# Down projection with stored activation sums: seven-product pairs at nine positions of each group instead of seven

## The chip, the cores and the metric

One Trainium2 chip, one of its cores. The metric is the device time of one execution in microseconds; lower is better. Engines: TensorE (PE, with its weight loads PEld), VectorE (DVE), ScalarE (ACT), GpSimd (POOL) and SyncE (SP); GpSimd and SyncE here mostly issue transfers.

## The reference

One layer (DEPTH 1) over 256 positions of width 2048, float32. A mixer comes first (its projection, gated chunks, neighbourhood attention, gates, output projection). Then a channel mixer, which is what the change touches, and a final norm:

```python
def conv_ffn(x, g_norm, w_up, conv_k, conv_b, w_down):      # D_FF = 5504, so 43 blocks of 128
    h = rms_norm(x, g_norm)
    up = h @ w_up                                            # 256 x 2048 by 2048 x 11008
    ...                                                      # centred depthwise convolution, width 3
    gate, val = jnp.split(up, 2, axis=-1)
    return x + (jax.nn.silu(gate) * val) @ w_down            # 256 x 5504 by 5504 x 2048
```

## The kernel before

**Products in two halves.** Every float32 operand is split into a high half (ScalarE copies it, rounding: `whi`, line 151) and a low half (VectorE subtracts the high half from the original: `wlo`, line 152). A product is a *triple* of matmuls (`triple`, lines 289 to 293): high by high, low by high, high by low.

**Order.** The schedule is written out by hand. All weights are a list of *pieces* that is worked from front to back. `begin(i)` opens piece `i`: it issues the load of the piece four further on (`load_to`, five `wraw` buffers, SyncE's queue, lines 126 and 132), splits the piece three further on (`split_to`, four `whi` and four `wlo` buffers), and runs the tasks registered for `i` with `at(i, f)`. Each engine works its instructions in the order in which they were issued this way, so a task that is put into a later piece stands behind that piece's splits. A tile that is allocated again under its name waits until its last reader is through.

**Up projection** (`g_up`, lines 199 to 221). 22 groups of eight pieces, weights stationary, two feature blocks (a *pair*, the last group one block) with gate and value in each. `ev_up` then brings the results out: banks to `ta` (lines 979 and 981), and as tasks convolution (987 to 994), SiLU and product (999 and 1000), and the split into the activation tile `a` (`split_plain`, 485 and 486). First block: one to three pieces after the group's end; second: three to five.

**Down projection** (`g_dn`, `wide`, `run_wide`). Two groups of 1024 output columns. A piece is one feature block (128 rows of `w_down`) by 1024 columns, two halves of 512; positions are two tiles of 128. A group has 43 pieces: 21 pairs of pieces at positions 0 to 20, and one left over. A *plain* pair takes 2 x 2 x 2 = 8 triples. At the positions in `DOWN_QUADS` the pair is done as a 2 x 2 block product with seven multiplications instead of eight (7 triples), by block sums of the activations and of the weights:

- `act_sums` (lines 295 to 304, five pieces ahead) adds the activation's halves back together and makes four block sums; `act_sums_split` (306 to 311, four ahead) splits them, into the tiles `h6` and `h7` of the pool `hT`.
- `weight_sums` (313 to 319, three ahead) makes four sums of the raw weight blocks, `weight_sums_split` (322 to 330, two ahead) splits them. Of the two pieces themselves, the first is then split only by half (`units`).
- The seven products go into the group's four banks and four banks of their own; `ev_sums` (899 to 922) adds the latter to the residual `x2` in two halves, `first_half` one piece and `second_half` two pieces after the last such pair.

The last four pieces of the second group are worked block by block (positions tile by column half, `tail` in `run_wide`), and `finish` ends each block: residual, squares, gain, and for each tile the norm and the output. `ev_down` ends the first group: residual, squares and gains of its columns, and `load_fin` (line 1272), which loads gains through GpSimd's queue into one of two buffers.

The same sums (`act_sums`, `weight_sums`, `post_sums`, `add_sums`) serve the four other places where seven products are used: the projection's `v` and values, the gates and the output projection.

Of the kernel before, what the change touches and what calls it, by code (L numbers as in the profile page):

```python
# [8 lines left out]
F32 = mybir.dt.float32  # L9
# [15 lines left out]
NF = DFF // 128  # L25
# [30 lines left out]
OUT_ORDER = (tuple(range(16)), (0, 1, 6, 7, 2, 3, 10, 11, 4, 5, 8, 9, 12, 13, 14, 15))  # L56
TURN_X2 = (13, 1)
Y_GAP = 224
DOWN_QUADS = ((4, 6, 9, 11, 14, 16, 18), (3, 5, 8, 10, 13, 15, 17))


@with_exitstack
def trunk_kernel(ctx, tc, x, norm_mix, w_in, ln_g, ln_b, w_s, b_s, rpb, w_branch, w_out,
# [200 lines left out]

    def wide(src, row0, order, c0, acts, quads, room, done, sums=None, odd=None):
        n0 = plan_wide(src, row0, order, c0)
        boxes = {}
        for n, q in enumerate(quads):  # L270
            i = n0 + 2 * q
            own = odd if odd and n % 2 else room
            whole[i] = whole[i + 1] = None
            units[i], units[i + 1] = 1, 2
            b = boxes[q] = {}
            if sums is None:
                b["acts"] = {}
                sum_acts_at(i - 5, i - 4, b["acts"], lambda k=order[2 * q]: ff["ap"][k // 2], room, "s")
            else:
                b["acts"] = sums[order[2 * q]]  # L280
            at(i - 3, lambda i=i, b=b: weight_sums(i, b, room))
            at(i - 2, lambda b=b, own=own: weight_sums_split(b, own))
        return ("wide", n0, order, acts, quads, boxes, done)
# [5 lines left out]
    def triple(p, x, h, l, st, sp):  # L289
# [2 lines left out]
        nc.tensor.matmul(p, xl, h, start=False, stop=False)  # L292
        nc.tensor.matmul(p, xh, l, start=False, stop=sp)  # L293

    def act_sums(a, box, room):
        w = room("f", F32)
        f = w[:, 0].rearrange("p (k t) -> p k t", k=2)
        nc.vector.tensor_add(f, a[:, :, 0, :].bitcast(F32), a[:, :, 1, :].bitcast(F32))
        s1, s2, s3, s4 = (w[:, 1, n * 128:(n + 1) * 128] for n in range(4))
        nc.vector.tensor_add(s1, f[:, 0, 128:], f[:, 1, 128:])  # L300
        nc.vector.tensor_sub(s3, f[:, 0, :128], f[:, 0, 128:])
        nc.vector.tensor_sub(s2, s1, f[:, 0, :128])
        nc.vector.tensor_sub(s4, f[:, 1, :128], s2)
        box["w"] = w

    def act_sums_split(box, room, name):
        w = box.pop("w")
        o = room(name, F32R)
        nc.scalar.activation(o[:, 0], w[:, 1], AF.Copy)
        nc.vector.tensor_sub(o[:, 1], w[:, 1], o[:, 0].bitcast(F32))  # L310
        box["s"] = [(o[:, 0, n * 128:(n + 1) * 128], o[:, 1, n * 128:(n + 1) * 128]) for n in range(4)]

    def weight_sums(i, box, room):
        r0, r1 = whole.pop(i), whole.pop(i + 1)
        t13, t24 = room("t13", F32), room("t24", F32)
        nc.vector.tensor_sub(t13[:, 0], r0[:, 1], r0[:, 0])
        nc.vector.tensor_sub(t24[:, 0], r1[:, 1], t13[:, 0])
        nc.vector.tensor_sub(t13[:, 1], r1[:, 1], r0[:, 1])
        nc.vector.tensor_sub(t24[:, 1], r1[:, 0], t24[:, 0])
        box["w"] = (t13, t24)  # L320

    def weight_sums_split(box, room):
        u = []
        for name, t in zip(("13", "24"), box.pop("w")):
            h, l = room("h" + name, F32R), room("l" + name, F32R)
            nc.scalar.activation(h, t, AF.Copy)
            nc.vector.tensor_sub(l, t, h.bitcast(F32))
            u.append((h, l))
        box["t"] = {1: [x[:, 0] for x in u[0]], 3: [x[:, 1] for x in u[0]],
                    2: [x[:, 0] for x in u[1]], 4: [x[:, 1] for x in u[1]]}  # L330

    def run_wide(g, tail=0):
        kind, n0, order, acts, quads, boxes, done = g
        n1 = n0 + len(order)
        P = C = None

        def x_of(k, t):
            a = acts(k)
            return a[:, 0, t * 128:(t + 1) * 128], a[:, 1, t * 128:(t + 1) * 128]

        def plain(i, t, c):
            h, l = split_t[i]
            triple(C[t][c], x_of(order[i - n0], t), h[:, c], l[:, c], i == n0, i == n1 - 1)

        for i in range(n0, n1 - tail):
            begin(i)
            q, r = divmod(i - n0, 2)
            if C is None:
                c = [bank() for _ in range(4)]
                C = [c[:2], c[2:]]  # L350
            if q not in quads:
                for t, c in ((0, 0), (0, 1), (1, 0), (1, 1)) if i > 1 else ((0, 0), (1, 0), (0, 1), (1, 1)):
                    plain(i, t, c)
                split_t.pop(i)
                continue
            st, sp = q == quads[0], q == quads[-1]
            k, k1 = order[2 * q:2 * q + 2]
            if r == 0:
                if st:
                    P = [bank() for _ in range(4)]  # L360
                (h0, l0), (h1, l1) = split_t[i], split_t[i + 1]
                triple(P[0], x_of(k, 0), h0[:, 0], l0[:, 0], st, sp)
                triple(C[0][0], x_of(k1, 0), h1[:, 0], l1[:, 0], False, False)
                triple(C[0][1], boxes[q]["acts"]["s"][3], h1[:, 1], l1[:, 1], False, False)
                split_t.pop(i)
                split_t.pop(i + 1)
                continue
            S, W = boxes[q]["acts"]["s"], boxes[q]["t"]
            triple(P[1], S[0], *W[1], st, sp)
            triple(P[3], S[2], *W[3], st, sp)  # L370
            triple(P[2], S[1], *W[2], st, sp)
            triple(C[1][0], x_of(k1, 1), *W[4], False, False)
            if sp:
                done[0](P, i)
        if not tail:
            done[1](C, n1)
            return
        for t in range(NT):
            for c in range(2):
                for i in range(n1 - tail, n1):  # L380
                    if t == 0 and c == 0:
                        begin(i)
                    plain(i, t, c)
                done[1](C, t, c)
# [140 lines left out]
    def post_sums(P, x, spare):  # L525
        p1, p5, p6, p7 = P
        (x11, x12), (x21, x22) = x
        nc.scalar.activation(x11, p1, AF.Copy)
        nc.vector.tensor_add(spare, p6, x11)
        nc.vector.tensor_add(x12, p5, spare)  # L530
        nc.vector.tensor_add(x21, p7, spare)
        nc.vector.tensor_add(x22, p5, x21)

    def add_sums(ps, x):
        for t in range(NT):
            for c in range(2):
                nc.vector.tensor_add(x[t][c], ps[t][c], x[t][c])

    def ev_v_sums(P, i):
        def go():  # L540
# [358 lines left out]
    def ev_sums(j, room):  # L899
        def done(P, i):  # L900
# [5 lines left out]
            def first_half():  # L906
                ab, cd = room("t13", F32), room("t24", F32)
                m["v"], m["u3"], m["w"] = cd[:, 0], cd[:, 1], ab[:, 0]
                nc.scalar.activation(ab[:, 0], p1, AF.Copy)
                nc.vector.tensor_add(x11, p1, x11)  # L910
                nc.vector.tensor_add(ab[:, 1], p6, ab[:, 0])
                nc.vector.tensor_add(m["v"], p5, ab[:, 1])
                nc.vector.tensor_add(m["u3"], p7, ab[:, 1])
                nc.vector.tensor_add(m["w"], p5, m["u3"])

            def second_half():
                nc.vector.tensor_add(x12, x12, m["v"])
                nc.vector.tensor_add(x21, x21, m["u3"])
                nc.vector.tensor_add(x22, x22, m["w"])

            at(i + 1, first_half)
            at(i + 2, second_half)
# [50 lines left out]
    def ev_up(f0, nb):  # L973
        def done(ps, i):
            n = nb
            a = []
            for p in ps:
                t = tmp.tile([128, T], F32, name="tb", bufs=3)
                nc.scalar.activation(t, p[:, T:], AF.Copy)  # L979
# [18 lines left out]
            def gate(b, g, v):  # L998
                nc.scalar.activation(g, g, AF.Silu)
                nc.vector.tensor_mul(g, g, v)  # L1000
                at(cur[0] + 1, lambda: split_plain(g, ff["a"][f0 + b]))

            at(i + 1, lambda: conv(0))
            if n > 1:
# [19 lines left out]
    def ev_down(ps, i):  # L1024
# [8 lines left out]
        def columns(j):  # L1033
            for t in range(NT):
                scale_columns(t, j)
            fin["load"]()

        for j in range(2):
            at(i + 2 + j, lambda j=j: squares(j))
# [93 lines left out]
    for f in range(0, NF, 2):  # L1133
        nb = min(2, NF - f)
        g_up.append(stationary(w_u, 0, KD, f * 128, nb * 128, 2, DFF, lambda k: rs["h", k], ev_up(f, nb)))
    h_room = {n: f"h{i}" for i, n in enumerate(("t13", "t24", "h13", "h24", "l13", "l24", "f", "s"))}

    def down_room(name, dt):
        return hpool.tile([128, 2, 512], dt, name=h_room[name])

    g_dn = [wide(w_d, 0, range(NF), g * 1024, lambda k: ff["a"][k], DOWN_QUADS[g], down_room,
                 (ev_sums(2 * g, down_room), ev_down if g == 0 else finish)) for g in range(2)]


    preload[0] = [lambda: load_x(0, 256)]
    for n, (c, _) in enumerate(X_TURN[1:]):
# [102 lines left out]
    ctx.push(fa_st)  # L1249
    ff["ap"] = [fa.tile([128, min(2, NF - k), 2, T], F32R, name=f"a{k // 2}") for k in range(0, NF, 2)]  # L1250
    ff["a"] = [ff["ap"][k // 2][:, k % 2] for k in range(NF)]
    fc = {}

    def open_conv():
# [54 lines left out]
```

## Time and profile before

| | |
|---|---|
| three runs, median | 1316.88 us (1316.34 to 1316.91) |
| profiled execution, span from first to last instruction | 1314.9 us; no other time of its own is given |
| mean granted TensorE clock | 0.998 |
| instructions | 19329 |
| weight transfers of the down projection, `in_w_down_dram` | 86 x 512 KB, median 4.6 us to landing |
| device memory read, written | 253.90 MB, 2.10 MB |

The span is about 2 us less than the runs' times. Rows of a profile table of windows give the stretch, its length, and then the busy time (and instructions) of PE, PEld, DVE, ACT and POOL, the granted clock, the transfer engines' share and GB/s. Rows of the timeline give start, duration, engine, line, operation, output<-inputs, shape, and in brackets the idle time before with what ended it. Rows of the waits give the waiting engine and line, what it waited for, and the time in all, the times and the longest. Durations of successive instructions on one engine overlap by about 0.1 us, so starts are the surer measure.

### The profile page before, as it was taken

What the parts mean: (1) busy time and instruction counts of PE and PEld (TensorE: products, weight loads), DVE (VectorE), ACT (ScalarE), POOL (GpSimd) and SP (SyncE); (2) the same over time, 40 slices, a digit from 0 to 9 for tenths busy, and PEclk for the clock granted to TensorE, in tenths of its full rate; (3) what the DMA queues carried; (4) which work ended last, traced back from release to release, by engine and by line L of the source; (5) the groups of instructions that cost most, each with busy time, mean ns of one, the idle gap of its engine ahead of it and who ended that gap; (6) DMA issues with size and microseconds to landing.
All of it is one profiled execution on the core that took longest, in us unless ns stands there. A gap on an engine that the chain in (4) does not pass through costs nothing.

```text
span 1314.9 us, 19329 instructions
## 1 busy us (share of the span) xinstructions
PE 1303.3 (99%) x6776; PEld 1112.0 (85%) x6776; DVE 1066.2 (81%) x1625; ACT 764.8 (58%) x1139; POOL 88.3 (7%) x176
## 2 busy tenths in 40 slices
PE   9999999999999999999999999999999999999997
PEld 7888888888888888888888888888888888888885
DVE  7996778667789966986777778787878789999997
ACT  5766476666645644556555555555656556555653
POOL 0004505323000000000000000000000000000000
PEclk9999999999999999999999999999999999999999
DMA  8768656556556657665565665656565656666663
GB/s 305 260 209 235 201 174 201 181 163 194 179 172 209 210 190 241 204 210 163 175 202 182 192 193 182 195 184 193 180 205 177 198 154 226 220 194 206 210 202 119
DMA packets 170577, 259.37 MB, mean 197 GB/s; under 512 B 12664, under 2 KB 124144, under 8 KB 170480
## 3 DMA queue, kind: packets, MB, share of 16 engines
q1 hardware_dynamic: 166448, 250.31, 59.4%
q0 software_dynamic: 3712, 7.30, 2.4%
q8 instruction: 53, 0.87, 0.3%
q10 hardware_dynamic: 320, 0.53, 0.1%
q14 instruction: 44, 0.36, 0.1%
HBM read 253.90 MB, written 2.10 MB: 195 GB/s over the span
## 4 chain that ended last, share of the span: by engine, by line
PE 97%; DVE 1%; ACT 0%; issue 0%; DMA 0%; ACTq 0%; DVEq 0%
PE bank L205 31%; PE bank L209 16%; PE bank L293 12%; PE bank L291 12%; PE bank L292 12%; PE bank L233 5%; PE bank L235 4%; PE bank L234 4%; PE bank L761 1%; DVE wlo L152 0%; PE bank L811 0%; PE bank L503 0%; PE bank L627 0%; PE bank L801 0%; PE bank L892 0%
## 5 line engine op out<-in xcount | busy, mean ns | idle before, releaser
L152 DVE TENSOR_TENSOR wlo<-wraw,whi 128x1024 fp32r<-128x1024 f32 (+1 forms) x472 | 550.3, 1178 | 188.7 <-ACT whi L151 92.0
L151 ACT ACTIVATE whi<-wraw 128x1024 fp32r<-128x1024 f32 (+1 forms) x472 | 472.0, 1015 | 204.7 <-PE bank L292 75.2
L205 PE MATMUL bank<-h,whi 128*128 128x512 f32 x1760 | 426.0, 392 | 0.0
L205 PEld LDWEIGHTS bank<-h,whi 128*128 128x128 f32 x1760 | 321.9, 188 | 62.0 <-DVE ya L631 0.3
L209 PEld LDWEIGHTS bank<-h,wlo 128*128 128x128 f32 x1760 | 225.9, 191 | 8.8
L209 PE MATMUL bank<-h,wlo 128*128 128x256 f32 x1760 | 228.6, 283 | 0.0
L989 ACT ACTIVATE tc<-ta,ck 128x256 f32<-128x256 f32 x86 | 47.1, 594 | 117.1 <-DVE ta L987 117.1
L293 PE MATMUL bank<-wlo,a 128*128 128x512 f32 x260 | 101.5, 390 | 0.2 <-DVE wlo L152 0.2
L292 PE MATMUL bank<-whi,a 128*128 128x512 f32 x260 | 101.2, 389 | 0.0
L291 PE MATMUL bank<-whi,a 128*128 128x512 f32 x260 | 101.2, 389 | 0.0
L291 PE MATMUL bank<-whi,h 128*128 128x512 f32 x204 | 80.3, 393 | 0.0
L292 PE MATMUL bank<-whi,h 128*128 128x512 f32 x204 | 79.5, 390 | 0.0
L293 PE MATMUL bank<-wlo,h 128*128 128x512 f32 x204 | 79.5, 390 | 0.0
L293 PEld LDWEIGHTS bank<-wlo,a 128*128 128x128 f32 x260 | 48.8, 188 | 11.2 <-DVE wlo L152 1.3
L292 PEld LDWEIGHTS bank<-whi,a 128*128 128x128 f32 x260 | 48.8, 188 | 10.3
L291 PEld LDWEIGHTS bank<-whi,a 128*128 128x128 f32 x260 | 48.8, 188 | 10.1
L992 DVE SCALAR_TENSOR_TENSOR tc<-ta,ck,tc 128x255 f32<-128x255 f32 x86 | 41.4, 481 | 14.5 <-ACT tc L989 14.5
L979 ACT ACTIVATE tb<-bank 128x256 f32<-128x256 f32 x86 | 28.3, 385 | 42.2 <-PE bank L205 42.2
L233 PE MATMUL bank<-whi,y 128*128 128x512 f32 x128 | 50.5, 394 | 0.0
L233 PE MATMUL bank<-whi,h 128*128 128x512 f32 x128 | 50.4, 394 | 0.0
L235 PE MATMUL bank<-wlo,h 128*128 128x512 f32 x128 | 49.9, 390 | 0.0
L235 PE MATMUL bank<-wlo,y 128*128 128x512 f32 x128 | 49.9, 390 | 0.0
(299 smaller groups left out, 1744.1 us busy)
## 6 DMA issues: line engine op xcount, KB each, us to landing
wraw<-in_w_up_dram SPq DMA_DIRECT2D x336, 256.0 KB, 3.2
wraw<-in_w_in_dram SPq DMA_DIRECT2D x111, 512.0 KB, 4.5
wraw<-in_w_down_dram SPq DMA_DIRECT2D x86, 512.0 KB, 4.6
wraw<-in_w_in_dram SPq DMA_DIRECT2D x66, 256.0 KB, 3.2
wraw<-in_w_branch_dram SPq DMA_DIRECT2D x32, 512.0 KB, 4.5
wraw<-in_w_out_dram SPq DMA_DIRECT2D x32, 512.0 KB, 3.6
xs<-in_x_dram SPq DMA_DIRECT2D x8, 256.0 KB, 7.6
vw<-y POOLq DMA_DIRECT2D x16, 128.0 KB, 6.9
```

Of the source, the lines that this page charges most:

```text
L151: nc.scalar.activation(h[:, k, :m], w[:, k, :m], AF.Copy)
L152: nc.vector.tensor_sub(l[:, k, :m], w[:, k, :m], h[:, k, :m].bitcast(F32))
L205: nc.tensor.matmul(p, h[:, k - k0, b * 128:(b + 1) * 128], acts(k), start=k == 0, stop=k == nk - 1)
L209: nc.tensor.matmul(p[:, :T], l[:, k - k0, b * 128:(b + 1) * 128], acts(k)[:, 0, :], start=False, stop=False)
L233: nc.tensor.matmul(p, xh, h[:, kk, :m], start=st, stop=False)
L234: nc.tensor.matmul(p, xl, h[:, kk, :m], start=False, stop=False)
L235: nc.tensor.matmul(p, xh, l[:, kk, :m], start=False, stop=sp)
L291: nc.tensor.matmul(p, xh, h, start=st, stop=False)
L292: nc.tensor.matmul(p, xl, h, start=False, stop=False)
L293: nc.tensor.matmul(p, xh, l, start=False, stop=sp)
L989: nc.scalar.activation(v, u, AF.Identity, scale=ck[:, 1, ch:ch + 1], bias=ck[:, 3, ch:ch + 1])
L992: nc.vector.scalar_tensor_tensor(v[:, 1:], u[:, :T - 1], ck[:, 0, ch:ch + 1], v[:, 1:], op0=OP.mult, op1=OP.add)
```

## The change

The block sums of the activations are no longer made in the down projection, once for each group. For nine pairs of feature blocks (3, 5, ... 19) they are made once, in the up projection: two pieces after the second block's gate VectorE makes the four sums from the unsplit product, one piece later they are split, and GpSimd's queue stores them in device memory (512 KB for each pair). The down projection loads them through the same queue, four pieces ahead of the pair, into `h6` and `h7` in turn. Both groups have nine seven-product pairs, at every second position; in the second group the blocks are put in another order, so that the stored pairs stand at its positions. The block sums are written with other signs (`act_blocks`, `weight_sums`), and the places that take them follow. The gain load after the first group is put three pieces later. GpSimd's descriptor space falls from its default to 4096 bytes a partition, and a pool `more` holds the sums on their way.

```diff
-DOWN_QUADS = ((4, 6, 9, 11, 14, 16, 18), (3, 5, 8, 10, 13, 15, 17))
+DOWN_PAIRS = (3, 5, 7, 9, 11, 13, 15, 17, 19)
+DOWN_QUADS = (DOWN_PAIRS, (2, 4, 6, 8, 10, 12, 14, 16, 18))
...
-            if sums is None:
+            if stored:
                 b["acts"] = {}
-                sum_acts_at(i - 5, i - 4, b["acts"], lambda k=order[2 * q]: ff["ap"][k // 2], room, "s")
+                at(i - 4, lambda b=b, k=order[2 * q]: stored(k // 2, b["acts"]))
...
+    def act_blocks(w, a11, a21, a12, a22):
+        s3, n1, p2, s4 = (w[:, n * 128:(n + 1) * 128] for n in range(4))
+        nc.vector.tensor_sub(s3, a11, a21)
+        nc.vector.tensor_sub(n1, a22, a21)
+        nc.vector.tensor_add(p2, n1, a11)
+        nc.vector.tensor_sub(s4, a12, p2)
...
-        nc.vector.tensor_sub(t13[:, 0], r0[:, 1], r0[:, 0])
-        nc.vector.tensor_sub(t24[:, 0], r1[:, 1], t13[:, 0])
-        nc.vector.tensor_sub(t13[:, 1], r1[:, 1], r0[:, 1])
-        nc.vector.tensor_sub(t24[:, 1], r1[:, 0], t24[:, 0])
+        nc.vector.tensor_add(t13[:, 0], r0[:, 0], r0[:, 1])
+        nc.vector.tensor_add(t24[:, 1], t13[:, 0], r1[:, 1])
+        nc.vector.tensor_add(t13[:, 1], r0[:, 1], r1[:, 1])
+        nc.vector.tensor_add(t24[:, 0], r1[:, 0], t24[:, 1])
...
-            triple(P[1], S[0], *W[1], st, sp)
-            triple(P[3], S[2], *W[3], st, sp)
-            triple(P[2], S[1], *W[2], st, sp)
+            triple(P[1], S[1], *W[1], st, sp)
+            triple(P[3], S[0], *W[3], st, sp)
+            triple(P[2], S[2], *W[2], st, sp)
...
                 at(cur[0] + 1, lambda: split_plain(g, ff["a"][f0 + b]))
+                own[b] = g
+                if b and f0 // 2 in ff["kept"]:
+                    at(cur[0] + 2, sums)
+                    at(cur[0] + 3, sums_split)
+
+            def sums():
+                own["w"] = ff["more"].tile([128, 512], F32, name="sw")
+                act_blocks(own["w"], *(own[k][:, t * 128:(t + 1) * 128] for k in range(2) for t in range(2)))
+
+            def sums_split():
+                o = ff["more"].tile([128, 2, 512], F32R, name="so")
+                split_plain(own["w"], o)
+                nc.gpsimd.dma_start(ff["kept"][f0 // 2], o.bitcast(F32))
...
-            fin["load"]()
+            at(cur[0] + 3, fin["load"])
...
-    h_room = {n: f"h{i}" for i, n in enumerate(("t13", "t24", "h13", "h24", "l13", "l24", "f", "s"))}
+    h_room = {n: f"h{i}" for i, n in enumerate(("t13", "t24", "h13", "h24", "l13", "l24", "s0", "s1"))}
...
-    g_dn = [wide(w_d, 0, range(NF), g * 1024, lambda k: ff["a"][k], DOWN_QUADS[g], down_room,
-                 (ev_sums(2 * g, down_room), ev_down if g == 0 else finish)) for g in range(2)]
+    def stored(pair, box):
+        n = ff["turn"] = ff.get("turn", -1) + 1
+        o = down_room(f"s{n % 2}", F32R)
+        nc.gpsimd.dma_start(o.bitcast(F32), ff["kept"][pair])
+        box["s"] = sums_of(o)
+
+    def down_order(g):
+        free = [p for p in range(NF // 2) if p not in DOWN_PAIRS]
+        kept = list(DOWN_PAIRS)
+        pairs = [(kept if q in DOWN_QUADS[g] else free).pop(0) for q in range(NF // 2)]
+        return tuple(2 * p + kk for p in pairs for kk in range(2)) + (NF - 1,)
+
+    g_dn = [wide(w_d, 0, down_order(g), g * 1024, lambda k: ff["a"][k], DOWN_QUADS[g], down_room,
+                 (ev_sums(2 * g, down_room), ev_down if g == 0 else finish), stored=stored) for g in range(2)]
+    dram = keep("dram", space=bass.MemoryType.DRAM)
+    ff["kept"] = {p: dram.tile([128, 2, 512], F32, name=f"sums{p}") for p in DOWN_PAIRS}
...
-    nc = _bacc.Bacc("TRN2", target_bir_lowering=False, num_devices=1)
+    nc = _bacc.Bacc("TRN2", target_bir_lowering=False, num_devices=1, dynamic_dma_scratch_size=4096)
```

The lines left out turn the signs where the sums are taken up (`post_sums`, `add_sums`, `ev_sums`: one subtraction for one addition), and divide `act_sums` into `act_blocks` and the rest.

More of the change, by code (lines that the diff above doesn't have):

```diff
@@ L262, in run_group, with wide @@
             done(ps, b)
-    def wide(src, row0, order, c0, acts, quads, room, done, sums=None, odd=None):
+    def wide(src, row0, order, c0, acts, quads, room, done, sums=None, odd=None, stored=None):
         n0 = plan_wide(src, row0, order, c0)
@@ L298, in act_sums @@
         nc.vector.tensor_add(f, a[:, :, 0, :].bitcast(F32), a[:, :, 1, :].bitcast(F32))
[L299 to L303, printed above, removed]
+        act_blocks(w[:, 1], *(f[:, k, t * 128:(t + 1) * 128] for k in range(2) for t in range(2)))
         box["w"] = w
@@ L310, in act_sums_split, with sums_of @@
         nc.vector.tensor_sub(o[:, 1], w[:, 1], o[:, 0].bitcast(F32))
-        box["s"] = [(o[:, 0, n * 128:(n + 1) * 128], o[:, 1, n * 128:(n + 1) * 128]) for n in range(4)]
+        box["s"] = sums_of(o)
+    def sums_of(o):
+        return [(o[:, 0, n * 128:(n + 1) * 128], o[:, 1, n * 128:(n + 1) * 128]) for n in range(4)]
     def weight_sums(i, box, room):
@@ L329, in weight_sums_split @@
         box["t"] = {1: [x[:, 0] for x in u[0]], 3: [x[:, 1] for x in u[0]],
-                    2: [x[:, 0] for x in u[1]], 4: [x[:, 1] for x in u[1]]}
+                    2: [x[:, 1] for x in u[1]], 4: [x[:, 0] for x in u[1]]}
     def run_wide(g, tail=0):
@@ L528, in post_sums @@
         nc.scalar.activation(x11, p1, AF.Copy)
-        nc.vector.tensor_add(spare, p6, x11)
+        nc.vector.tensor_sub(spare, x11, p6)
         nc.vector.tensor_add(x12, p5, spare)
@@ L536, in add_sums @@
             for c in range(2):
-                nc.vector.tensor_add(x[t][c], ps[t][c], x[t][c])
+                (nc.vector.tensor_sub if c else nc.vector.tensor_add)(x[t][c], ps[t][c], x[t][c])
     def ev_v_sums(P, i):
@@ L910, in first_half @@
                 nc.vector.tensor_add(x11, p1, x11)
-                nc.vector.tensor_add(ab[:, 1], p6, ab[:, 0])
+                nc.vector.tensor_sub(ab[:, 1], ab[:, 0], p6)
                 nc.vector.tensor_add(m["v"], p5, ab[:, 1])
@@ L916, in second_half @@
             def second_half():
-                nc.vector.tensor_add(x12, x12, m["v"])
+                nc.vector.tensor_sub(x12, x12, m["v"])
                 nc.vector.tensor_add(x21, x21, m["u3"])
-                nc.vector.tensor_add(x22, x22, m["w"])
+                nc.vector.tensor_sub(x22, x22, m["w"])
             at(i + 1, first_half)
@@ L976, in done @@
             a = []
+            own = {}
             for p in ps:
@@ L1135, in trunk_kernel @@
         g_up.append(stationary(w_u, 0, KD, f * 128, nb * 128, 2, DFF, lambda k: rs["h", k], ev_up(f, nb)))
-    h_room = {n: f"h{i}" for i, n in enumerate(("t13", "t24", "h13", "h24", "l13", "l24", "f", "s"))}
+    h_room = {n: f"h{i}" for i, n in enumerate(("t13", "t24", "h13", "h24", "l13", "l24", "s0", "s1"))}
     def down_room(name, dt):
         return hpool.tile([128, 2, 512], dt, name=h_room[name])
-    g_dn = [wide(w_d, 0, range(NF), g * 1024, lambda k: ff["a"][k], DOWN_QUADS[g], down_room,
-                 (ev_sums(2 * g, down_room), ev_down if g == 0 else finish)) for g in range(2)]
+    def stored(pair, box):
+        n = ff["turn"] = ff.get("turn", -1) + 1
+        o = down_room(f"s{n % 2}", F32R)
+        nc.gpsimd.dma_start(o.bitcast(F32), ff["kept"][pair])
+        box["s"] = sums_of(o)
+    def down_order(g):
[7 more added lines that the diff above has]
+    ff["kept"] = {p: dram.tile([128, 2, 512], F32, name=f"sums{p}") for p in DOWN_PAIRS}
     preload[0] = [lambda: load_x(0, 256)]
@@ L1251, in trunk_kernel @@
     ff["a"] = [ff["ap"][k // 2][:, k % 2] for k in range(NF)]
+    ff["more"], more_st = pool("more")
+    ctx.push(more_st)
     fc = {}
```

## The prediction
> **What bounds the kernel now.** I read the page's busy times and chain first, then a table of two windows (up projection, down projection), then what the matmul and weight-load queues wait for in each.
>
> ```profile
> PE 1303.3 (99%) x6776; PEld 1112.0 (85%) x6776; DVE 1066.2 (81%) x1625; ACT 764.8 (58%) x1139; POOL 88.3 (7%) x176
> PE 97%; DVE 1%; ACT 0%; issue 0%; DMA 0%; ACTq 0%; DVEq 0%
> ...
> 606.00:1080.00 474.00, 474.00 (x2730) 419.02 (x2729) 364.78 (x602) 271.76 (x436) 0.00 (x0) 1.00 0.59 185
> 1080.00:1315.00 235.00, 225.58 (x992) 185.61 (x991) 218.87 (x323) 128.59 (x162) 2.21 (x4) 0.99 0.60 198
> ...
> PEld bank L293 <- DVE wlo L152: 1.3, 3, 0.6
> PE bank L293 <- DVE wlo L152: 0.2, 1, 0.2
> ```
>
> TensorE is 97% of the chain. The last two rows are all it waits for from 1080 us on, and between 606 and 1080 it waits for nothing. The window rows give the room beside it: VectorE has 109 us left of 474 in the up projection (77% busy), but is 93% busy in the down projection. So matmuls taken out of the down projection count in full, as long as VectorE's low halves still arrive ahead of them. A busy matmul row overlaps the next one, so I take the pace from starts instead: these rows are the first matmul of the pair at position 4 and of the pair at position 6, the first two seven-product pairs, with one plain pair between.
>
> ```profile
> 1103.63 0.39 PE L291 MATMUL bank<-whi,h 128*128 128x512 f32 x1
> 1113.83 0.39 PE L291 MATMUL bank<-whi,h 128*128 128x512 f32 x1
> ```
>
> A seven-product pair has 7 triples, a plain pair 8: 21 + 24 = 45 matmuls in 10.20 us, 0.2267 us each.
>
> **Term 1, the matmuls.** Seven-product pairs go from 7 + 7 to 9 + 9. Four more pairs, one triple less each: 12 x 0.2267 = 2.72 us off TensorE. The other groups keep their matmuls; only signs change there, at one instruction for one (the block sums in `act_blocks` have one more back-to-back dependence, 0.1 us each time on VectorE, hidden).
>
> **Term 2, VectorE and ScalarE in the down projection.** Starts in order, from 1093.67 us:
>
> ```profile
> 1093.67 0.68 DVE L298 TENSOR_TENSOR h<-a 128x512 f32<-128x512 f32 x1
> 1094.39 0.29 DVE L300 TENSOR_TENSOR h<-h 128x128 f32<-128x128 f32 x1
> ...
> 1095.33 0.42 DVE L486 TENSOR_TENSOR a<-tc,a 128x256 fp32r<-128x256 f32 x1
> 1096.80 0.69 DVE L310 TENSOR_TENSOR h<-h,h 128x512 fp32r<-128x512 f32 x1
> 1097.40 0.69 DVE L152 TENSOR_TENSOR wlo<-wraw,whi 128x512 fp32r<-128x512 f32 x1
> 1098.00 0.69 DVE L316 TENSOR_TENSOR h<-wraw 128x512 f32<-128x512 f32 x1
> ...
> 1100.54 1.22 DVE L152 TENSOR_TENSOR wlo<-wraw,whi 128x1024 fp32r<-128x1024 f32 x1
> 1101.68 2.35 DVE L327 TENSOR_TENSOR h<-h,h 128x1024 fp32r<-128x1024 f32 x2
> 1103.95 1.22 DVE L152 TENSOR_TENSOR wlo<-wraw,whi 128x1024 fp32r<-128x1024 f32 x1
> ```
>
> From start to start: activation sums 1.66 us and their split 0.60 (together 2.26); half split of a weight piece 0.60, full split 1.14, weight sums 2.54, their split 2.27. Removed: 14 x 2.26 = 31.6 us. Added: four more pairs at 2.54 + 2.27 + 0.60 - 1.14 = 4.27, 17.1 us. VectorE's load there falls by 14.5 us. What matters is the densest stretch, a seven-product pair and a plain pair in turn: 0.60 + 2.54 + 1.14 + 2.27 + 2 x 1.14 = 8.83 us against TensorE's 10.20. With the sums in place the same stretch costs 11.09 today, over TensorE's time, and is made good where two plain pairs follow. So the nine pairs are the easier load for VectorE. ScalarE does one copy for each split and has more room still (128.59 of 235). Cost on the path: nothing, cover 1.4 us in each 10.2.
>
> **Term 3, the up projection.** Nine times VectorE does the four block sums (0.94 from 1094.39 to 1095.33, near 1.05 with the extra dependence) and a split of 0.60: 9 x 1.65 = 15 us in a stretch where it has 109 us left. They are queued two and three pieces after the gate, where only weight splits stand beside them: 1.14 + 1.05 a piece, against about 2.8 us of TensorE for a piece (64 high products of 0.2267 and as many half-width low ones in eight pieces). Behind them on VectorE are the next low halves, which stand up to three pieces ahead. ScalarE adds nine 128x512 copies. Nothing on the path. The nine stores wait on GpSimd's queue, which has nothing else there (0.00 in that window).
>
> **Term 4, the 18 loads.** They go through GpSimd's queue. The nearest rows are the residual's loads of the same size and, for the issue, the last gain load:
>
> ```profile
> x<-in_x_dram POOLq DMA_DIRECT2D x4, 512.0 KB, 7.8
> 1092.91 0.57 POOL L1272 DMA_DIRECT2D gfin<-in_norm_final_dram  x1 [577.36 <-DVE tc L1000]
> 1092.53 1.22 DVE L152 TENSOR_TENSOR wlo<-wraw,whi 128x1024 fp32r<-128x1024 f32 x1
> ```
>
> A slot is used by every other stored pair, so it comes free four pairs earlier and there lie a plain, a seven-product and a plain pair between: 69 x 0.2267 = 15.6 us, and 1.4 us more to the first triple that reads it. 0.6 + 7.8 us fit into 17 twice. The gain loads that stand in the same queue wait for VectorE's multiplies; their call has been moved three pieces on so that they do not hold up a stored load. GpSimd's issue at 1092.91 lies inside a VectorE split that took its usual 1.22 us, so an issue costs VectorE nothing that shows. The Trainium skill ("SBUF — State Buffer", Who interferes with whom) says that a VectorE instruction with two SBUF inputs contends with a GpSimd instruction that reads SBUF, and the loser blocks; by that, 18 issues of 0.57 us would take 10 us of VectorE, still inside 18 x 1.4 us. The trace's unstretched 1.22 us speaks against even that.
>
> **Term 5, the last four pieces.** They are worked block by block, so their last low half is wanted soon after its buffer comes free. First and last of these 48 matmuls, and what held two of them:
>
> ```profile
> 1288.47 0.68 DVE L910 TENSOR_TENSOR x<-bank,x 128x512 f32<-128x512 f32 x1
> 1291.72 1.22 DVE L152 TENSOR_TENSOR wlo<-wraw,whi 128x1024 fp32r<-128x1024 f32 x1
> 1292.85 0.69 DVE L917 TENSOR_TENSOR x<-x,h 128x512 f32<-128x512 f32 x1
> 1294.65 2.35 DVE L152 TENSOR_TENSOR wlo<-wraw,whi 128x1024 fp32r<-128x1024 f32 x2
> 1294.00 1.07 ACT L151 ACTIVATE whi<-wraw 128x1024 fp32r<-128x1024 f32 x1 [1.66 <-PE bank L292]
> ...
> 1294.03 0.39 PE L291 MATMUL bank<-whi,a 128*128 128x512 f32 x1
> 1297.07 0.50 PE L293 MATMUL bank<-wlo,a 128*128 128x512 f32 x1 [0.17 <-DVE wlo L152]
> 1305.36 0.39 PE L293 MATMUL bank<-wlo,a 128*128 128x512 f32 x1
> ```
>
> 47 x 0.2267 = 10.65 us, but first to last took 11.33: 0.68 us lost, because the second half of the sums (1292.85 to 1294.65) stands ahead of the last two splits. After, the last seven-product pair is position 18 instead of 17, so that second half is queued behind the last split and only the first half (3.25 us, 1288.47 to 1291.72) ahead of it. With TensorE at piece 38's start as zero: pair 18's products end at -0.7; split 41 ends near 0.75, the first half near 4.0; ScalarE's copy for piece 42 runs from 2.75 (its buffer) to 3.8; the last split ends near 5.2, and TensorE wants it at 5.2. So 0.6 of the 0.68 us goes, or, if VectorE arrives later than this, none. Next late is that same split. After the last matmul the ending stays as it is.
>
> **Term 6, the start of the down projection.** The first pair is at position 3 instead of 4, piece 6. VectorE has finished the gate and is free for it at 1092.53 (the split shown there becomes the half one): weight sums to 1095.7, last activation split to 1096.0, split 7 to 1097.15, sums' splits 1098.3 and 1099.4. TensorE reaches piece 6 here:
>
> ```profile
> 1096.83 0.39 PE L291 MATMUL bank<-whi,a 128*128 128x512 f32 x1
> ...
> L126 SPq DMA_DIRECT2D wraw<-in_w_down_dram x2: 328/328/328, 1085.0 to 1087.1; - x2
> wraw<-in_w_down_dram SPq DMA_DIRECT2D x12, 512.0 KB, 5.6
> ...
> 1080.00:1100.00 20.00, 20.00 (x88) 16.28 (x88) 19.09 (x35) 12.85 (x20) 1.13 (x2) 1.00 0.83 259
> ```
>
> It wants low half 7 five matmuls later, 1097.96, and the sums' low halves at 1099.3 and 1100.7: 0.8 us of slack at the least, no cost. The weights of piece 7, issued at 1085.0, land about 5.6 us later, 1090.6; the second weight sum wants them at 1093.85.
>
> **Sum.** -2.72 - 0.6 = -3.3 us on a span of 1314.9. The profiled execution has no time of its own beside its span; the three runs (1316.34 to 1316.91) lie about 2 us above it, as start and end would on any run of this program, so the shift goes on the median: 1316.88 - 3.3 = 1313.6. About 0.2%, 2.6 us, is what a measurement of this kernel can tell from no change; the forecast is 0.25%, just over.
>
> **Rivals.**
> 1. The tail keeps its loss: -2.7, 1314.2, on the edge of the bound. For it: the last split above has no slack. Chance 0.12.
> 2. The first two stored loads crowd the weights. They are issued as soon as the up projection's last matmuls free their slots, near 1080, where the transfers already run at 0.83 of their engines and 259 GB/s (row above); 1.05 MB at that rate is 4.0 us. Piece 7's weights have 3.25 + 0.8 = 4.0 us of cover. If the loads come wholly ahead of them and land slower than that, TensorE stalls 0.5 to 2.5 us: 1314.1 to 1316.1. The Trainium skill ("DMA: Bandwidth & Descriptors", Issuing engines are not separate DMA queues) says that transfers from all queues run on the same engines and interleave, so the second queue brings no bandwidth; by it the crowding is real. Against it: interleaving also means a share of the delay only. Chance 0.18.
> 3. Slower: a stored pair lands late each time. The place is the triple that reads its fourth sum; it decides once a load takes over 17 us from the slot's release, twice the 8.4 of the rows. At 20 us each of the 14 loads that reuse a slot within a group would hold TensorE 3 us, 42 us in all: 1356. At 17.5 it would be 7 us, 1320.6. For it: the loads read device memory beside weights at 198 GB/s. Against it: 18 x 0.52 MB over 235 us is 40 GB/s more, some 0.12 of the engines' time, on 0.60. Chance 0.07.
> 4. The change does not save what it says, because the higher density makes weights wait for raw buffers held for the sums: pairs two positions apart stand in this trace already (4 and 6, 14 to 18) without a transfer wait. No gain, 1316.9. Chance 0.03.
>
> **How the numbers follow.** Forecast 0.60. Faster: 0.60, half of rival 1 and a little of 2, 0.68. Same: the rest of 1 and 2 with 4, 0.24. Slower: 0.08. The range begins 0.7 us under the forecast (the tail's and the start's last tenths, and the runs' own spread of 0.57) and reaches over rivals 1, 2 and 4 to 1317.0.
>
> **What would show it.** Right: 12 matmuls fewer, 0.2267 us apart throughout; no wait on GpSimd's transfers in TensorE's list; VectorE near 204 of 232 us in the down projection, its idle time now before weight splits that wait for a buffer; the last 48 matmuls in 10.7 us. Wrong: a wait of line 291 to 293 for a transfer (rival 3), a hole near pieces 6 to 8 (rival 2), any wait in the up projection, or low halves still last in the tail (rival 1).

## The result and the profile after

Seven runs each on one chip: 1313.29 us median (1312.90 to 1313.69) against 1316.88 (1316.32 to 1317.30), 3.59 us less; ratio 0.9973 with a 95% interval of 0.9963 to 0.9984. The profiled execution after has a span of 1311.9 us and took 1313.69 itself. Among the runs of the experiments further down one stands apart: seven of e5's eight took 1312.80 to 1313.64 us and one took 2646.81; nothing on record explains it, and no reading here rests on it.

The page's busy times and chain, the two windows (stretch, length, then busy time and instructions of PE, PEld, DVE, ACT, POOL, granted clock, transfer share, GB/s), and all that TensorE and its weight loads wait for in the down projection:

```profile
PE 1300.6 (99%) x6764; PEld 1110.6 (85%) x6764; DVE 1067.4 (81%) x1610; ACT 770.7 (59%) x1142; POOL 103.3 (8%) x203
PE 98%; DVE 1%; ACT 0%; issue 0%; DMA 0%; ACTq 0%; DVEq 0%
606.00:1080.00 474.00, 474.00 (x2732) 418.99 (x2731) 378.28 (x646) 277.10 (x444) 4.87 (x9) 1.00 0.62 195
1080.00:1311.90 231.90, 222.75 (x984) 183.85 (x982) 206.35 (x264) 129.21 (x156) 11.70 (x22) 0.99 0.70 242
PEld bank L294 <- DVE wlo L153: 0.3, 1, 0.3
```

12 matmuls fewer (6764 for 6776). VectorE gives 12.5 us back in the down projection (218.87 to 206.35) and takes 13.5 in the up projection (364.78 to 378.28), where TensorE is still busy throughout. Of the 1.3 us that the weight loads waited for low halves 0.3 is left, and the matmul queue's own wait is gone.

The first and the last matmul of the down projection, and the first of its last 48, give its length. In this kernel the lines of `triple` and of the splits are one further on (292 to 294, 152 and 153), those after them up to 36.

```profile
1080.67 0.39 PE L292 MATMUL bank<-whi,a 128*128 128x512 f32 x1
...
1291.69 0.39 PE L292 MATMUL bank<-whi,a 128*128 128x512 f32 x1
1302.37 0.39 PE L294 MATMUL bank<-wlo,a 128*128 128x512 f32 x1
```

Before, the same three are at 1080.30, 1294.03 and 1305.36; the prediction shows the last two, and the first is:

```profile
1080.30 0.39 PE L291 MATMUL bank<-whi,a 128*128 128x512 f32 x1
```

From first to last: 225.06 us before, 221.70 after, 3.36 less; the last 48 took 11.33 and now take 10.68. The down projection begins 0.37 us later in this profile, a shift that is there by 108 us, long before anything the change adds; over the profiles below this start lies anywhere from 1079.90 to 1081.66. So the length of the down projection is the surer measure, and I use it beside the medians.

### The profile page after: what moved, and what is told of

Its sections match the earlier page's. It is cut to its first block, busy times and chain, and to the rows that moved or that the text cites. A ratio compares the mean times of both kernels' runs of the same rounds, so it can differ in the third digit from the quotient of the medians.

```text
span 1311.9 us, 19400 instructions
## 1 busy us (share of the span) xinstructions
PE 1300.6 (99%) x6764; PEld 1110.6 (85%) x6764; DVE 1067.4 (81%) x1610; ACT 770.7 (59%) x1142; POOL 103.3 (8%) x203
## 4 chain that ended last, share of the span: by engine, by line
PE 98%; DVE 1%; ACT 0%; issue 0%; DMA 0%; ACTq 0%; DVEq 0%
PE bank L206 31%; PE bank L210 16%; PE bank L292 12%; PE bank L294 12%; PE bank L293 12%; PE bank L234 5%; PE bank L236 4%; PE bank L235 4%; PE bank L768 1%; PE bank L818 0%; PE bank L510 0%; PE bank L634 0%; PE bank L808 0%; PE bank L971 0%; PE bank L899 0%
## 5 line engine op out<-in xcount | busy, mean ns | idle before, releaser
L294 PE MATMUL bank<-wlo,a 128*128 128x512 f32 x236 | 91.9, 390 | 0.0
L293 PE MATMUL bank<-whi,a 128*128 128x512 f32 x236 | 91.8, 389 | 0.0
L292 PE MATMUL bank<-whi,a 128*128 128x512 f32 x236 | 91.8, 389 | 0.0
L292 PE MATMUL bank<-whi,h 128*128 128x512 f32 x208 | 82.3, 396 | 0.0
L293 PE MATMUL bank<-whi,h 128*128 128x512 f32 x208 | 81.3, 391 | 0.0
L333 ACT ACTIVATE h<-h 128x1024 fp32r<-128x1024 f32 x36 | 36.2, 1052 | 36.4 <-DVE h L325 19.7
L294 PEld LDWEIGHTS bank<-wlo,a 128*128 128x128 f32 x236 | 44.3, 188 | 9.6 <-DVE wlo L153 0.3
L292 PEld LDWEIGHTS bank<-whi,a 128*128 128x128 f32 x236 | 44.3, 188 | 9.2
L293 PEld LDWEIGHTS bank<-whi,a 128*128 128x128 f32 x236 | 44.3, 188 | 9.1
L234 PE MATMUL bank<-whi,h 128*128 128x512 f32 x128 | 50.4, 394 | 0.0
```

Source lines behind the costliest of these rows:

```text
L234: nc.tensor.matmul(p, xh, h[:, kk, :m], start=st, stop=False)
L292: nc.tensor.matmul(p, xh, h, start=st, stop=False)
```

## The experiments

One table for all; lengths are first to last matmul of the down projection and of its last 48, medians are the runs', each beside the kernel before on its own chip.

| kernel | pairs, sums | median, us | before there | ratio (95%) | down, us | last 48, us |
|---|---|---|---|---|---|---|
| before | 7 + 7, in place | 1316.88 | | | 225.06 | 11.33 |
| the change | 9 + 9, stored | 1313.29 | 1316.88 | 0.9973 (0.9963 to 0.9984) | 221.70 | 10.68 |
| e1_seven_stored | 7 + 7, stored | 1316.00 | 1316.58 | 0.9996 (0.9987 to 1.0004) | 224.41 | 10.68 |
| e2_nine_in_place | 9 + 9, in place | 1339.11 | 1316.58 | 1.0170 (1.0156 to 1.0184) | 248.24 | 14.59 |
| e3_eight | 8 + 8, stored | 1314.76 | 1316.58 | 0.9985 (0.9976 to 0.9994) | 223.02 | 10.67 |
| e4_nine_to_17 | 9 + 9, second to 17 | 1313.45 | 1316.58 | 0.9975 (0.9965 to 0.9985) | 221.67 | 10.68 |
| e5_double_loads | 9 + 9, loaded twice | 1313.29 | 1316.65 | 0.9974 (0.9964 to 0.9985) | 221.68 | 10.67 |
| e6_sp_queue | 9 + 9, SyncE's queue | 1312.93 | 1316.65 | 0.9974 (0.9964 to 0.9984) | 221.66 | 10.66 |
| e7_store_only | 7 + 7, in place, stores unread | 1317.49 | 1316.65 | 1.0007 (0.9998 to 1.0016) | 225.21 | 11.45 |
| e8_one_slot | 9 + 9, one slot | 1318.09 | 1316.65 | 1.0010 (1.0001 to 1.0019) | 225.92 | 10.65 |
| e9_ten | 9 + 10, stored | 1312.66 | 1316.64 | 0.9971 (0.9960 to 0.9983) | 221.07 | 10.75 |
| e9_change_again | the change | 1313.46 | 1316.64 | 0.9975 (0.9966 to 0.9984) | 221.67 | 10.69 |

**e1: the storing without the extra pairs.**

```diff
-DOWN_PAIRS = (3, 5, 7, 9, 11, 13, 15, 17, 19)
-DOWN_QUADS = (DOWN_PAIRS, (2, 4, 6, 8, 10, 12, 14, 16, 18))
+DOWN_PAIRS = (4, 6, 9, 11, 14, 16, 18)
+DOWN_QUADS = (DOWN_PAIRS, (3, 5, 8, 10, 13, 15, 17))
```

> Sums stored and loaded as in the change, but at the old positions: 7 and 7 pairs, the second group's last at 17. No matmul is saved, VectorE is relieved by 31.6 us in the down projection. My theory of the tail (the second half of the last pair's sums is queued ahead of the last two splits when that pair stands at 17) says the tail keeps its 0.68 us: 1316.9, the 48 last matmuls in 11.3 us. Rival for the tail (VectorE came to the tail late because of its backlog, and a relieved VectorE is in time at any position): 1316.2, 48 matmuls in 10.7 us. Rival for the whole gain (it comes from relieving VectorE and not from the matmuls): 1314 or less.

The down projection is 0.65 us shorter and the tail's loss is gone with the last pair still at 17. (By the medians alone, 0.58 us with an interval that includes no difference, this could not be told.) My theory of the tail falls; the rival, backlog, fits. The rival for the whole gain falls too: VectorE is relieved more than in the change, and the median is 2.7 us above it. VectorE's end of the second group in this kernel shows it:

```profile
1283.58 3.50 DVE L153 TENSOR_TENSOR wlo<-wraw,whi 128x1024 fp32r<-128x1024 f32 x3 [1.30 <-ACT whi L152]
1286.99 0.68 DVE L917 TENSOR_TENSOR x<-bank,x 128x512 f32<-128x512 f32 x1
...
1291.01 1.23 DVE L153 TENSOR_TENSOR wlo<-wraw,whi 128x1024 fp32r<-128x1024 f32 x1 [0.69 <-ACT whi L152]
1292.15 0.68 DVE L924 TENSOR_TENSOR x<-x,h 128x512 f32<-128x512 f32 x1
...
1293.96 1.22 DVE L153 TENSOR_TENSOR wlo<-wraw,whi 128x1024 fp32r<-128x1024 f32 x1
1296.45 1.23 DVE L153 TENSOR_TENSOR wlo<-wraw,whi 128x1024 fp32r<-128x1024 f32 x1 [1.27 <-ACT whi L152]
1298.32 0.69 DVE L1035 TENSOR_TENSOR x<-bank,x 128x512 f32<-128x512 f32 x1 [0.64 <-PE bank L294]
...
1295.39 0.39 PE L292 MATMUL bank<-whi,a 128*128 128x512 f32 x1
```

The second half of the sums (from 1292.15) is ahead of the last two splits here as well. But the first half began at 1286.99, and the tail's first matmul (the last row) is at 1295.39: 8.4 us between. Before, from 1288.47 to 1294.03, there were 5.6. VectorE now waits before the last split for ScalarE's copy (1.27 us idle), where before it came straight from the split ahead of it.

**e2: the extra pairs without the storing.**

```diff
-                at(i - 4, lambda b=b, k=order[2 * q]: stored(k // 2, b["acts"]))
+                sum_acts_at(i - 5, i - 4, b["acts"], lambda k=order[2 * q]: ff["ap"][k // 2], room, "s1")
...
-                if b and f0 // 2 in ff["kept"]:
+                if False:
...
-    h_room = {n: f"h{i}" for i, n in enumerate(("t13", "t24", "h13", "h24", "l13", "l24", "s0", "s1"))}
+    h_room = {n: f"h{i}" for i, n in enumerate(("t13", "t24", "h13", "h24", "l13", "l24", "f", "s1"))}
```

> Nine and nine pairs at the change's positions, but the activation sums made in the down projection as before (five pieces ahead), nothing stored or loaded. 12 matmuls less as in the change. My theory (VectorE then needs 11.09 us for each 10.20 us of TensorE, 8 times in each group, and has some 1 to 3 us of lead): TensorE waits for low halves and sums, 4 to 6 us in each group, 1322 to 1326. Rival (the stored sums were not needed, VectorE has room): as the change, 1313.3 to 1313.6.

The direction is as expected, the size is not: 22.5 us over the kernel before. Its down projection by the window, 40 us from the middle of its first group, and the waits of TensorE and of VectorE for TensorE:

```profile
1080.00:1338.00 258.00, 230.99 (x980) 184.33 (x978) 245.45 (x371) 135.38 (x174) 2.20 (x4) 0.98 0.56 181
1120.00:1160.00 40.00, 37.20 (x160) 29.54 (x159) 39.55 (x57) 21.94 (x25) 0.00 (x0) 1.00 0.57 186
...
PEld bank L294 <- DVE wlo L153: 25.8, 19, 4.0
PE bank L294 <- DVE wlo L153: 17.8, 17, 3.6
DVE x L1035 <- PE bank L294: 1.8, 1, 1.8
```

VectorE's whole work there is 245.45 us (241.2 of it in the 248.5 us up to the last matmul) against 222 us that TensorE needs. It is held up by its own work and not by buffers: it is busy 39.55 of the 40 us shown, and waits for TensorE once, 1.8 us. I had added up only what each dense stretch loses (0.9 us, eight times) and left out that the group's other work on VectorE (the gate's tail, the sums' two halves, the residual and gain columns) lives from the same room. Once VectorE is the bound, all of its work counts. 12 matmuls fewer cost 22.5 us when the sums stay in place.

**e3: eight pairs.** `DOWN_PAIRS` 3 to 17 and the second group 4 to 18, nothing else.

> Stored sums with eight and eight pairs (3 to 17, 4 to 18): 6 matmuls more than the change, its tail unchanged. My theory (0.2267 us for each matmul, nothing else): 1313.3 + 1.36 = 1314.65. Rival (the gain is VectorE's relief): 1313.3 or less, since VectorE has still less to do.

1314.76, and the down projection 1.32 us longer than the change's: six matmuls at 0.22 us. The gain goes by the matmul, and less work on VectorE does not make up for it.

**e4: the second group one position earlier.** `(1, 3, 5, 7, 9, 11, 13, 15, 17)` for its positions.

> The change with the second group's nine pairs one position earlier, 1 to 17 instead of 2 to 18. My theory of the tail (position): the second half of the sums is ahead of the last two splits again, 0.6 us lost, 1313.9, the 48 last matmuls in 11.3 us. Rival (backlog): VectorE is as relieved as in the change, no loss, 1313.3, 10.7 us.

No loss: 10.68 us for the last 48 and the change's time. With e1 this shows that position 17 costs nothing once VectorE is relieved: the loss needs its backlog. Whether position 18 would have removed the loss under the old load is not tried.

**e5: every stored pair loaded twice**, the second time into a tile that nothing reads.

```diff
         nc.gpsimd.dma_start(o.bitcast(F32), ff["kept"][pair])
+        nc.gpsimd.dma_start(ff["more"].tile([128, 2, 512], F32R, name="so").bitcast(F32), ff["kept"][pair])
```

> The change with every stored pair loaded twice, the second time into a spare tile that nothing reads: 9.4 MB more through the same queue. My theory (the transfers lie inside their covers: 17 us for a stored pair, 4.0 us for the first weights, of which the crowding took about 1.9): 1313.3 within 0.5, weights of the down projection land 0.5 to 2 us later. Rival (the change is already near the limit of the transfers): a hole near pieces 6 to 8 or waits for transfers, 1315 to 1320.

No difference. Its transfers in the down projection (queue, count, size, median us to landing), and its window:

```profile
wraw<-in_w_down_dram SPq DMA_DIRECT2D x80, 512.0 KB, 5.5
h<-sums POOLq DMA_DIRECT2D x18, 512.0 KB, 7.1
so<-sums POOLq DMA_DIRECT2D x18, 512.0 KB, 8.6
...
1080.00:1311.40 231.40, 222.28 (x980) 183.50 (x978) 206.07 (x263) 128.93 (x156) 20.93 (x40) 0.99 0.79 283
```

Weights land after 5.5 us, in the change after 5.0, before after 4.6: the transfers do crowd each other, but the covers hold at 283 GB/s.

**e6: the loads in SyncE's queue**, `nc.sync` for `nc.gpsimd` in `stored`.

> The change with the stored pairs loaded through SyncE's queue, between the weight loads, instead of GpSimd's. Each then waits in that queue until TensorE has left its slot, and the weight loads behind it wait too, by my count 1 to 2 us, inside some 5 us of their cover: 1313.3 within 0.5. Rival (a queue of their own is needed, since weights behind a waiting load come late): TensorE or VectorE waits for weights, 1315 to 1325.

The same time within the runs' spread. The queue's own waits for the slots, and the loads themselves:

```profile
SPq L1165 <- PE bank L294: 15.9, 14, 1.6
...
h<-sums SPq DMA_DIRECT2D x18, 512.0 KB, 5.8
```

The stored loads hold the weight queue 1.1 us on average, 1.6 at most, as counted, and nothing downstream notices. They land after 5.8 us in the median, against 7.0 through GpSimd's queue in the change.

**e7: the up projection's part alone.** The change's sums and stores, with the old positions, the old order and sums in place.

> The up projection's part alone: sums of nine pairs made and stored there, but never loaded; the down projection makes its own sums and has the old seven and seven pairs in the old order. My theory (15 us of VectorE and nine stores lie in the up projection's idle time): as before, 1316.6 to 1316.9. Rival (they cost): each group of the up projection that makes sums is longer than 22.27 us, 1317.5 or more.

0.84 us over the kernel before, with an interval that includes no difference (0.9998 to 1.0016), and outside what I expected. The trace shows 0.15 of it, in the down projection, where the block sums in place have one more dependence (argued, not tried). The up projection itself is not longer: from the last square block (L964 before, L971 here) to the first down matmul it is 1080.30 less 605.72 = 474.58 us before and 1080.72 less 606.14 = 474.58 here. Most of the 0.84 lies outside the span from first to last instruction: over this kernel's eleven runs 2.2 to 2.5 us lie outside it (median 2.4), over the 27 of the kernel before on the same chip 1.7 to 1.9, while the spans' medians, 1315.2 and 1314.9, are 0.3 apart. What these 0.65 us are stays open; the change, with the same sums and stores, does not have them (1.8).

**e8: one slot instead of two.** `down_room("s0", F32R)` for `down_room(f"s{n % 2}", F32R)`.

> The change with one slot for the stored pairs instead of two: a pair's load then starts when the pair before it has been read, 33 matmuls (7.5 us) ahead of its own use, against 0.5 + 7.0 us for issue and landing. This tries the price of a late stored pair. My theory (the cover decides, and is now used up): TensorE waits 0 to 1.5 us at most of 16 pairs, 1316 to 1328. Rival (loads are far faster when less crowded, or the cover is not what counts): 1313.3 within 0.5.

```profile
PEld bank L292 <- DMA h<-sums: 4.9, 6, 2.5
PE bank L292 <- DMA h<-sums: 2.8, 3, 2.1
PEld bank L294 <- DVE wlo L153: 0.3, 1, 0.3
```

4.8 us over the change and 4.2 in the down projection, in six waits for the transfer of the sums; I had expected waits at most of 16 pairs. The loads take 4.3 to 9.2 us to land here. This is the prediction's slower rival in a small form: with 7.5 us of cover some loads come late, with 17 none do. The second slot is worth more than the 12 matmuls.

**e9: ten pairs in the second group**, on one chip with the change once more.

```diff
-DOWN_PAIRS = (3, 5, 7, 9, 11, 13, 15, 17, 19)
-DOWN_QUADS = (DOWN_PAIRS, (2, 4, 6, 8, 10, 12, 14, 16, 18))
+DOWN_PAIRS = (1, 3, 5, 7, 9, 11, 13, 15, 17, 19)
+DOWN_QUADS = (DOWN_PAIRS[1:], (1, 3, 5, 7, 9, 11, 13, 15, 16, 18))
...
-        free = [p for p in range(NF // 2) if p not in DOWN_PAIRS]
-        kept = list(DOWN_PAIRS)
+        kept = list(DOWN_PAIRS[-len(DOWN_QUADS[g]):])
+        free = [p for p in range(NF // 2) if p not in kept]
```

> Ten pairs are stored, and the second group does ten: positions 1, 3, ... 15, 16, 18, so two stand side by side; the first group keeps nine. 3 matmuls less than the change. My theory (0.2267 us a matmul while VectorE is relieved): 0.68 us less than the change on the same chip, 1312.6. Rival (side by side does not work: the split sums of pair 16 can only be written once TensorE has left pair 15, and all later low halves stand behind them): TensorE waits 0.5 to 4 us there, 1313.3 to 1317.

> The changed kernel once more, for comparison on the same chip: 1313.3, as recorded.

1312.66 against 1313.46, and 221.07 us against 221.67 in the down projection. Two pairs side by side do work once, and the 0.6 us are three matmuls less about 0.1 that comes back in the tail:

```profile
PEld bank L294 <- DVE wlo L153: 0.5, 2, 0.3
```

It is the fastest of these kernels by the median; 0.8 us is inside the intervals of the ratios, so the length of the down projection carries that reading, one profile of each; between the change's two profiles it differs by 0.03 us.

## Why the prediction was right, step by step

**The sum.** -3.3 us was forecast and -3.59 measured by the medians (-3.36 in the down projection); 1313.6 against 1313.29. The 0.23 us between the two measures is less than the spread of the seven runs (0.79).

**Term 1** holds: 12 matmuls at 0.2267 us, 2.72 us; without its last 48 matmuls the down projection took 213.73 us and now takes 211.02, 2.71 less. e3 has the same price for six.

**Term 2** holds in size: 12.5 us off VectorE's busy time for 14.5 worked out. The stretch of a seven-product and a plain pair in the change, from one pair's first weight sum to the next's:

```profile
1102.65 0.68 DVE L323 TENSOR_TENSOR h<-wraw 128x512 f32<-128x512 f32 x1
...
1111.46 0.68 DVE L323 TENSOR_TENSOR h<-wraw 128x512 f32<-128x512 f32 x1
```

8.81 us, for 8.83 worked out. What the step undersold is how much hangs on it: e2 shows the same twelve matmuls turned into a loss of 22.5 us without it.

**Term 3** holds: 13.5 us of VectorE for 15, nothing on TensorE's path.

**Term 4** holds. The 18 loads and nine stores, and the shortest, median and longest time of a load to landing:

```profile
h<-sums POOLq DMA_DIRECT2D x18, 512.0 KB, 7.0
sums<-so POOLq DMA_DIRECT2D x9, 512.0 KB, 4.3
...
DMA to landing us min/median/max: 5.1/7.0/8.7
```

No load took over 8.7 us, half of the 17 at which rival 3 begins. The Trainium skill's rule on VectorE and GpSimd ("SBUF — State Buffer", Who interferes with whom) is one for GpSimd instructions that read SBUF, and the prediction stretched it to issues. It leaves no mark here: an issue lies inside a run of splits that keeps its usual pace.

```profile
1101.75 0.53 POOL L1165 DMA_DIRECT2D h<-sums  x1 [4.46 <-PE bank L294]
1099.78 2.95 DVE L153 TENSOR_TENSOR wlo<-wraw,whi 128x1024 fp32r<-128x1024 f32 x3
```

2.95 us are two full splits and a half one (1.14 + 1.14 + 0.68); a block of 0.53 us would show.

**Term 5 has the right size and an incomplete reason.** 0.65 us went, 0.6 was forecast. The step that failed is "because the second half of the sums stands ahead of the last two splits": e1 and e4 keep it there and lose nothing. The loss needed VectorE to reach the first half late, a backlog that it carried along, and the relief of term 2 is enough to remove it. Under the old load the order may have mattered as well. In the prediction's rows the last split begins near 1295.8 (1294.65 and a full split), straight behind the one ahead of it and 0.7 us after ScalarE's copy for it was through (1294.00 + 1.07); without the second half's 1.8 us it could have begun with the end of the copy. That is an estimate from those rows; no run has position 18 with the old load. So the forecast of 0.6 us rested on a step that was not needed, and that its size came out is in part luck. Rival 1 was priced by that order alone.

**Term 6 and rival 2** hold. The weight loads at the start of the down projection (1079.5 to 1094 us), before and then after, count, size and median us to landing:

```profile
wraw<-in_w_down_dram SPq DMA_DIRECT2D x7, 512.0 KB, 5.9
```

```profile
wraw<-in_w_down_dram SPq DMA_DIRECT2D x6, 512.0 KB, 7.1
h<-sums POOLq DMA_DIRECT2D x2, 512.0 KB, 8.0
```

The crowding is there, 1.2 us of it in the median (1.9, from 5.4 to 7.3, in the one load behind the figure in e5's expectation), as the Trainium skill's rule says ("DMA: Bandwidth & Descriptors", Issuing engines are not separate DMA queues). It lies inside the 4.0 us of cover: VectorE's second weight sum starts straight behind the first.

```profile
1093.50 0.68 DVE L323 TENSOR_TENSOR h<-wraw 128x512 f32<-128x512 f32 x1
1094.22 0.69 DVE L324 TENSOR_TENSOR h<-h,wraw 128x512 f32<-128x512 f32 x1
```

TensorE's one wait of 0.3 us at the start of the down projection was there before too.

Rival 4 falls with the 12 matmuls measured in full.

## What to carry to other kernels

When one engine is the bound and the next one is at 93%, moving the second one's work to a stretch where it has room is what lets the first be relieved: here neither half does it alone (e1 -0.6 us, e2 +22.5, together -3.6). Count the second engine's whole work against the first's, not only its densest stretch, and ask of any small wait near the end whether a backlog brought it there. The reload from device memory was free here while its slot came free early enough (17 us, at up to 283 GB/s) and was not with 7.5 us, so count the slots before the bytes.

## What was not expected

Doubling the reloads (283 GB/s in the down projection) moved nothing, while taking one slot away cost 4.8 us. And the start of the down projection moved by up to 1.8 us between the profiles above, about half of the whole effect, through small waits long before the change's stretch. One of them, in e1, whose down projection began last:

```profile
PEld bank L206 <- DVE ya L638: 1.5, 1, 1.5
```

So a sub-percent change is better read from its own stretch than from one span.
